# Latent attention in a two-layer decoder: rotation of all tokens of two heads on VectorE instead of GpSimd, rotary scores as stacked high and low parts, the causal mask by TensorE

## The chip, the core and the metric

One core of a Trainium2 chip runs the whole program in one launch. The metric is the device time of one execution in microseconds (us); the time before is the median of three runs. The core has TensorE (matrix products, `T` in the code, PE in the profile), VectorE (`V`, DVE), ScalarE (`A`, ACT), GpSimd (`G`, POOL) and SyncE (`Q`, SP), which issues most of the transfers. The engines run side by side, each working through its own queue in order.

## The reference

A sequence of 512 tokens of width 1024 goes through two layers, each of which is SwiGLU, a token mixer beside a memory cross-attention, and SwiGLU again. The mixer of the first layer is gated linear attention; that of the second is multi-head latent attention (MLA), and all of the change lies there:

```python
q = (rmsnorm(c_q, q_norm) @ w_uq).reshape(B, S, 8, 128 + 64)
kv = (rmsnorm(c_kv, kv_norm) @ w_ukv).reshape(B, S, 8, 128 + 128)
q_nope = rmsnorm(q[..., :128], qn_norm)
q_rope = apply_rope(rmsnorm(q[..., 128:], qr_norm), cos, sin)
k_nope = rmsnorm(kv[..., :128], kn_norm)
k_rope = apply_rope(rmsnorm(k_r, kr_norm)[:, :, None, :], cos, sin)   # one for all heads
# apply_rope: t1, t2 = halves of 32;  [t1*c - t2*s, t1*s + t2*c]
s = (q_nope k_nope + q_rope k_rope) * 192 ** -0.5;  causal mask;  softmax;  times v
```

All arithmetic is float32.

## The kernel before, in words

**Arithmetic.** Large products are made of float32r operands (a float32 rounded so that TensorE takes it in one pass): each operand is split into a high part and what is left (a low part), and `mm3` adds three products. Weights come by DMA as `raw`, ScalarE rounds them into `wh`, VectorE subtracts to make `wl`. Small products (attention scores, probabilities times values) use plain float32 operands; each such product stands in the trace as two matmul records.

**The MLA mixer** (`mla`, line 1387). The latents `cq`, `ck` and the raw rotary key `krn` come from token projections; `rope_tables` makes eight tables of cosines and sines times gains on GpSimd. `rope_key` (line 1437) rotates the key of all 512 tokens, copies it into both halves of 128 columns, and transposes it, so that `kr["t"]` holds it twice, on rows 0 to 63 and 64 to 127.

Then come four pairs of heads, pair 0 to pair 3. For each pair TensorE projects keys and values (four blocks of 128 tokens, 512 wide) and queries (four blocks, 384 wide: 256 without position, 128 rotary). `query` copies a block out of PSUM and sums its squares, `queries` (line 1477) waits for all four blocks, takes the inverse roots, and for each block j scales its two parts on VectorE and calls `rotate` (line 1373), six GpSimd instructions of 64 elements. Then each block takes three transposes, two for the heads and one for both rotary parts. `attend` (line 1540) makes the scores of one head and block j as a float32 product over 128 rows and a second one over the 64 rows of that head's rotary part, both `(j+1)*128` wide, and `attention` (line 1107) adds the mask to the diagonal block in PSUM on VectorE, takes the row maximum, the exponential on ScalarE, scales the rows, transposes, and multiplies by the values. When pair 2 is through its projections, `mem.attend`, the cross-attention into the memory tokens, is started too. After pair 3's projections the output projection `project_out` (line 873) begins with the first six heads: each of its eight outputs needs heads 0 to 5 in order, so it can't finish one before pair 2 is through its attention.

**What sets the order.** The kernel is written as generators ("flows"), and a planner (`Flows.run`, line 264) picks in each step the flow whose next instruction can start first by its own cost table (`Engine.price`, line 142). The order so found is fixed at build time: each engine's queue has it, and an instruction that waits holds up all behind it. The flows take temporary tiles from a pool of 33 tiles of 1024 columns, most of them as halves of 512 (`tt`), banks of PSUM from eight. All engine calls are made on line 138, so the profile's rows are told apart by tiles and shapes: `cs` with a PE row is the identity, so `ps<-cs,t` is a transpose; `t,wh` is the output projection or SwiGLU; `wh,t` with 384 or 512 columns is a pair's projection; `ps<-t` is attention; `cm` with a DVE row holds the mask, `s` are columns of sums.

Of the kernel before, what the change touches and what calls it, by code (L numbers as in the profile page):

```python
# [9 lines left out]
F32 = mybir.dt.float32  # L10
# [279 lines left out]
def _emit(tc, ctx, xT, memT, wflat, sizes, cst, out):  # L290
# [816 lines left out]
    def attention(scores, blocks, value, o, mask=None):  # L1107
# [265 lines left out]
    def rotate(dst, src, tabs, n):  # L1373

        tmp = yield tt()
        a, b, a2, b2 = (tmp[:, i * 128 : i * 128 + n].rearrange("p (x d) -> p x d", d=32) for i in range(4))
        c1, s1, c2, s2 = tabs
        t1, t2 = src[:, :, 0:32], src[:, :, 32:64]
        yield G.tensor_tensor(out=a, in0=t1, in1=c1, op=ALU.mult)
        yield G.tensor_tensor(out=b, in0=t2, in1=s2, op=ALU.mult)  # L1380
        yield G.tensor_tensor(out=dst[:, :, 0:32], in0=a, in1=b, op=ALU.subtract)
        yield G.tensor_tensor(out=a2, in0=t1, in1=s1, op=ALU.mult)
        yield G.tensor_tensor(out=b2, in0=t2, in1=c2, op=ALU.mult)
        yield G.tensor_tensor(out=dst[:, :, 32:64], in0=a2, in1=b2, op=ALU.add)
        done(tmp)

    def mla(l, nrm, nxt):
# [6 lines left out]
        yield from rope_tables(rt)  # L1394
        spawn(mem_prep(l, mem.mp))
# [41 lines left out]
        def rope_key():  # L1437
# [4 lines left out]
            yield from rotate(krd3[:, :, 0:ROPE], krn3, rt[4:8], 128)  # L1442
            yield G.tensor_copy(out=krd3[:, :, ROPE:], in_=krd3[:, :, :ROPE])
# [4 lines left out]
            kr["t"] = yield tt()  # L1448
            yield A.copy(out=kr["t"], in_=ps)
# [14 lines left out]
        def query(st, j, ps):  # L1464
            t = yield tt()
            yield A.copy(out=t[:, :384], in_=ps[:, :384])
# [7 lines left out]
            st["raw"][j] = t  # L1474
            st["f"][j].set = True

        def queries(st):
            for f in st["f"]:
                yield f
            ss, rc = st["ss"], small(16)  # L1480
            yield V.tensor_tensor(out=ss, in0=ss, in1=C("invq"), op=ALU.mult)
            yield from rsqrt(rc, ss, 1.0, 16)
            st["q"] = []
            for _ in range(3):
                st["q"].append((yield tt()))
            q0, q1, qr = st["q"]
            for j in range(NJ):
                qn = st["raw"][j]
                for c0, c1, dd, cc in ((0, 256, NOPE, 4 * j), (256, 384, ROPE, 4 * j + 2)):
                    q3 = heads(qn[:, c0:c1], 2)  # L1490
                    yield V.tensor_tensor(out=q3, in0=q3, in1=rc[:, cc : cc + 2].unsqueeze(2).to_broadcast([P, 2, dd]),
                                          op=ALU.mult)
                tabs = [rt[i][:, j, :].unsqueeze(1).to_broadcast([P, 2, 32]) for i in range(4)]
                yield from rotate(heads(qn[:, 384:512], 2), heads(qn[:, 256:384], 2), tabs, 64)
            for j in range(NJ):
                qn = st["raw"][j]
                pt = yield bank()
                for i, c0 in enumerate((0, 128, 384)):
                    yield T.transpose(out=pt[:, i * P : (i + 1) * P], in_=qn[:, c0 : c0 + P], identity=ident)
                done(qn)  # L1500
                sl = slice(j * P, (j + 1) * P)
                for i in range(2):
                    yield A.activation(out=st["q"][i][:, sl], in_=pt[:, i * P : (i + 1) * P], func=AF.Identity, scale=qns)
                yield V.tensor_copy(out=qr[:, sl], in_=pt[:, 2 * P : 3 * P])
                done(pt)
            st["qf"].set = True
# [11 lines left out]
        def keys(st):  # L1518
# [4 lines left out]
            st["k"] = []  # L1523
            for _ in range(2):
                st["k"].append((yield tt()))
            for j in range(NJ):
# [6 lines left out]
                for i in range(2):  # L1533
                    yield A.activation(out=st["k"][i][:, sl], in_=pt[:, i * P : (i + 1) * P], func=AF.Identity,
                                       scale=C("kn"))
# [4 lines left out]
        def attend(st, i, h):  # L1540
# [5 lines left out]
            rp = slice(i * ROPE, (i + 1) * ROPE)  # L1546

            def scores(ps, j):
                n = (j + 1) * P
                sl = slice(j * P, n)  # L1550
                yield T.matmul(ps[:, :n], lhsT=st["q"][i][:, sl], rhs=st["k"][i][:, :n], start=True, stop=False)
                yield T.matmul(ps[:, :n], lhsT=st["q"][2][rp, sl], rhs=kr["t"][rp, :n], start=False, stop=True)
# [253 lines left out]
```

## Time and profile before

| | us |
|---|---|
| median of three runs | 2018.53 (2016.92 to 2018.84) |
| profiled execution, its own time | 2016.53 |
| its span, first to last instruction | 2014.7 |
| PE busy in the span | 1999.7 |
| DVE busy | 1578.5 |
| ACT busy | 978.3 |
| POOL busy | 48.4 |

The span is one profiled execution. A row of instructions names line, engine, operation, out<-in tiles, shapes and count, then busy time and the mean duration of one in ns, then the idle time of the engine just before them with what ended it. Durations of matmuls overlap, so what one costs a full queue is read from start to start.

### The profile page before, as it was taken

The numbers are of one execution on the slowest core, as the hardware profiler recorded it, in microseconds if no ns is written. First come the engines' busy times: TensorE is split into PE (matmuls) and PEld (weight loads), VectorE is DVE, ScalarE is ACT, GpSimd is POOL, SyncE is SP. The second block draws the span as 40 slices with busy tenths as digits, with TensorE's granted clock in tenths as the row PEclk, the third lists the DMA queues.
The fourth block names the chain that finished last, engine by engine and source line by source line (L and its number), as shares of the span: only waits on it lengthen the run. The fifth ranks groups of instructions, "written<-read, shape, count | busy, mean of one in ns | idle before, by whom it ended". The sixth has DMA issues, their size and how long they took to land.

```text
span 2014.7 us, 32006 instructions
## 1 busy us (share of the span) xinstructions
PE 1999.7 (99%) x12862; PEld 1796.6 (89%) x12862; DVE 1578.5 (78%) x2573; ACT 978.3 (49%) x1574; POOL 48.4 (2%) x121
## 2 busy tenths in 40 slices
PE   9999999999999999999999999999999999999999
PEld 8999998878987899999899999989877779998997
DVE  8977786548776998678799777865887669987782
ACT  6543444444442664445565444444576456543451
POOL 0000000000000000000000000010031100000000
PEclk9999999999999999999999999999999999999999
DMA  5333333313212133323323333333210212332231
GB/s 180 108 108 102 105 105 112 108 63 105 74 57 79 64 97 114 115 86 104 126 96 105 105 105 100 101 115 111 87 45 32 84 43 84 105 128 92 95 126 63
DMA packets 55589, 193.22 MB, mean 96 GB/s; under 512 B 6160, under 2 KB 7824, under 8 KB 55440
## 3 DMA queue, kind: packets, MB, share of 16 engines
q1 hardware_dynamic: 55152, 189.92, 28.6%
q8 instruction: 101, 1.65, 0.3%
q10 hardware_dynamic: 288, 1.26, 0.2%
q14 instruction: 48, 0.39, 0.1%
HBM read 189.05 MB, written 2.10 MB: 95 GB/s over the span
## 4 chain that ended last, share of the span: by engine, by line
PE 87%; DVE 9%; ACT 2%; issue 1%; DMA 0%; POOL 0%; SPq 0%; ACTq 0%; DVEq 0%; POOLq 0%
PE ps L138 87%; DVE t L138 5%; DVE wl L138 2%; DVE s L138 2%; ACT t L138 1%; ACT wh L138 1%; DMA raw<-wflat 0%; DVE raw L138 0%; DVE x L138 0%; POOL t L138 0%; SPq L138 0%; DVE ps L138 0%; DVE rs L138 0%; ACTq L138 0%; DVEq L138 0%
## 5 line engine op out<-in xcount | busy, mean ns | idle before, releaser
L138 PE MATMUL ps<-t,wh 128*128 128x256 f32 (+1 forms) x6880 | 1528.0, 318 | 2.8 <-ACT wh L138 1.7
L138 PEld LDWEIGHTS ps<-t,wh 128*128 128x128 f32 x6880 | 1141.1, 191 | 96.0 <-issue 7.2
L138 PE MATMUL ps<-t,wl 128*128 128x256 f32 (+1 forms) x3440 | 1091.1, 317 | 0.1
L138 PEld LDWEIGHTS ps<-t,wl 128*128 128x128 f32 x3440 | 655.5, 191 | 45.6 <-issue 3.0
L138 ACT CAST wh<-raw 128x1024 fp32r<-128x1024 f32 (+2 forms) x358 | 368.6, 1031 | 483.8 <-PE ps L138 357.1
L138 DVE TENSOR_TENSOR wl<-raw,wh 128x1024 fp32r<-128x1024 f32 (+2 forms) x358 | 428.4, 1199 | 114.3 <-ACT wh L138 113.6
L138 DVE TENSOR_TENSOR t<-t 128x512 f32<-128x512 f32 (+3 forms) x514 | 306.5, 618 | 13.1 <-ACT t L138 8.4
L138 ACT CAST wh<-t 128x1024 fp32r<-128x1024 f32 x126 | 132.4, 1051 | 185.5 <-PE ps L138 98.9
L138 PE MATMUL ps<-wh,t 128*128 128x256 f32 (+3 forms) x928 | 214.9, 321 | 0.0
L138 DVE TENSOR_TENSOR wl<-t,wh 128x1024 fp32r<-128x1024 f32 x126 | 153.7, 1220 | 48.9 <-ACT wh L138 48.8
L138 DVE SCALAR_TENSOR_TENSOR x<-ps,x 128x512 f32<-128x512 f32 x160 | 109.8, 686 | 104.7 <-PE ps L138 104.6
L138 ACT COPY t<-ps 128x512 f32<-128x512 f32 (+3 forms) x262 | 138.8, 534 | 65.1 <-PE ps L138 58.5
L138 PEld LDWEIGHTS ps<-wh,t 128*128 128x128 f32 x928 | 155.1, 190 | 9.6 <-issue 2.2
L138 DVE TENSOR_TENSOR t<-ps,t 128x512 f32<-128x512 f32 (+2 forms) x191 | 122.6, 645 | 50.3 <-PE ps L138 36.0
L138 PE MATMUL ps<-wl,t 128*128 128x256 f32 (+3 forms) x464 | 148.2, 319 | 0.0
L138 PE MATMUL ps<-t 128*128 128x128 f32 (+6 forms) x760 | 139.7, 328 | 0.8 <-ACT t L138 0.4
L138 ACT CAST t<-t 128x256 fp32r<-128x256 f32 (+1 forms) x196 | 95.3, 509 | 78.8 <-DVE t L138 78.5
L138 PEld LDWEIGHTS ps<-t 128*128 128x128 f32 (+1 forms) x760 | 97.9, 190 | 30.4 <-issue 15.9
L138 DVE SCALAR_TENSOR_TENSOR t<-t 128x512 f32<-128x512 f32 (+1 forms) x168 | 106.0, 636 | 16.9 <-ACT t L138 16.2
L138 DVE TENSOR_TENSOR t<-t,raw 128x1024 f32<-128x1024 f32 x84 | 102.2, 1217 | 0.1
L138 ACT ACTIVATE t<-t 128x512 f32<-128x512 f32 x124 | 76.3, 629 | 48.1 <-DVE t L138 47.8
L138 PEld LDWEIGHTS ps<-wl,t 128*128 128x128 f32 x464 | 88.3, 190 | 4.9 <-issue 0.9
(76 smaller groups left out, 786.4 us busy)
## 6 DMA issues: line engine op xcount, KB each, us to landing
raw<-wflat SPq DMA_DIRECT2D x342, 512.0 KB, 3.3
raw<-wflat SPq DMA_DIRECT2D x12, 192.0 KB, 2.3
x<-xT SPq DMA_DIRECT2D x8, 256.0 KB, 5.6
t<-memT SPq DMA_DIRECT2D x8, 256.0 KB, 3.6
out<-x SPq DMA_DIRECT2D x8, 256.0 KB, 2.0
raw<-wflat SPq DMA_DIRECT2D x4, 448.0 KB, 3.3
cm<-cst ACTq DMA_DIRECT2D x1, 640.0 KB, 3.9
cm<-cst ACTq DMA_DIRECT2D x1, 585.5 KB, 4.2
```

The costliest lines, as they stand in the source:

```text
L138: return Op(self.name, lambda: real(*args, **kw), cost, _places(ins), _places(outs), lat)
```

## The change

- `rotate` runs on VectorE. It takes all four blocks of both heads of a pair in one call: four multiplications and two sums of 256 elements in place of 24 GpSimd instructions of 64. For the key it is six instructions of 128 elements, and the copy into the second half is VectorE's too.
- `query` puts the rotary parts of all blocks into one tile `st["rope"]`; one instruction reduces the six sums of a block, and the mean of a head's 128 columns is made from two sums of 64. The scaling of the rotary part is one instruction of 512 elements.
- The rotated queries are split into a rounded high part (ScalarE) and a low part (VectorE), which lie beside each other, 64 and 64 columns for each head, so that a transpose gives 128 rows: high above low. There are four transposes for a block in place of three.
- The rotated key is split into a pair of float32r tiles. The rotary score of a head is two float32r products over 128 rows, stacked query times high key and stacked query times low key, in place of one float32 product over 64 rows.
- The mask is added by a third product, identity times mask, 128 wide in float32r; the VectorE addition goes. Two casts at the start of `mla` make both operands.
- Both heads' queries and keys lie in whole tiles (`Take("d", ...)`), so that one ScalarE instruction of 256 elements scales both heads of a block; the VectorE copy of the rotary part is 256 wide instead of 128.

```diff
     def attention(scores, blocks, value, o):
         def rows(j, ps):
-            if mask is not None:
-                sl = slice(j * P, (j + 1) * P)
-                yield V.tensor_tensor(out=ps[:, sl], in0=ps[:, sl], in1=mask, op=ALU.add)
-    def rotate(dst, src, tabs, n):
-        yield G.tensor_tensor(out=a, in0=t1, in1=c1, op=ALU.mult)
...
-        yield G.tensor_tensor(out=dst[:, :, 32:64], in0=a2, in1=b2, op=ALU.add)
+    def rotate(dst, src, rt, n):
+        a, b = (t[:, : NJ * n * ROPE].rearrange("p (j h d) -> p j h d", j=NJ, h=n) for t in ab)
+        t1, t2 = src[:, :, :, 0:32], src[:, :, :, 32:64]
+        for out_, in_, i in ((a[:, :, :, 0:32], t1, 0), (b[:, :, :, 0:32], t2, 3), (a[:, :, :, 32:64], t2, 2),
+                             (b[:, :, :, 32:64], t1, 1)):
+            yield V.tensor_tensor(out=out_, in0=in_, in1=tab(i), op=ALU.mult)
+        yield V.tensor_tensor(out=dst[:, :, :, 0:32], in0=a[:, :, :, 0:32], in1=b[:, :, :, 0:32], op=ALU.subtract)
+        yield V.tensor_tensor(out=dst[:, :, :, 32:64], in0=a[:, :, :, 32:64], in1=b[:, :, :, 32:64], op=ALU.add)
     def mla(l, nrm, nxt):
+        yield V.tensor_copy(out=identr, in_=ident)
+        yield V.tensor_copy(out=maskr, in_=C("cmask"))
         def rope_key():
-            yield G.tensor_copy(out=krd3[:, :, ROPE:], in_=krd3[:, :, :ROPE])
+            yield V.tensor_copy(out=krd3[:, :, ROPE:], in_=krd3[:, :, :ROPE])
-            yield A.copy(out=kr["t"], in_=ps)
+            kr["t"] = yield from pair()
+            yield from split(ps, *kr["t"])
         def query(st, j, ps):
-            yield A.copy(out=t[:, :384], in_=ps[:, :384])
+            yield A.copy(out=t, in_=ps[:, :256])
+            yield A.copy(out=heads(st["rope"], NJ)[:, j, :], in_=ps[:, 256:384])
-            yield V.tensor_reduce(out=ss[:, 4 * j : 4 * j + 2], in_=heads(sq[:, :256], 2), op=ALU.add, axis=AX.X)
-            yield V.tensor_reduce(out=ss[:, 4 * j + 2 : 4 * j + 4], in_=heads(sq[:, 256:384], 2), op=ALU.add, axis=AX.X)
+            yield V.tensor_reduce(out=ss[:, 6 * j : 6 * j + 6], in_=heads(sq[:, :384], 6), op=ALU.add, axis=AX.X)
         def queries(st):
-                yield from rotate(heads(qn[:, 384:512], 2), heads(qn[:, 256:384], 2), tabs, 64)
+            yield V.tensor_tensor(out=q3, in0=q3, in1=rc6[:, :, 4:6].unsqueeze(3).to_broadcast([P, NJ, 2, ROPE]),
+                                  op=ALU.mult)
+            yield from rotate(ql, q3, rt, 2)
+            yield A.copy(out=qh.bitcast(F32R), in_=ql)
+            yield V.tensor_tensor(out=ql, in0=ql, in1=qh, op=ALU.subtract)
...
-                for i, c0 in enumerate((0, 128, 384)):
-                    yield T.transpose(out=pt[:, i * P : (i + 1) * P], in_=qn[:, c0 : c0 + P], identity=ident)
+                yield from transposes(pt, qn, 2)
+                for i in range(2):
+                    x = (2 * j + i) * P
+                    yield T.transpose(out=pt[:, (2 + i) * P : (3 + i) * P], in_=hl[:, x : x + P], identity=ident)
-                yield V.tensor_copy(out=qr[:, sl], in_=pt[:, 2 * P : 3 * P])
+                yield V.tensor_copy(out=heads(st["qr"], 2)[:, :, sl], in_=heads(pt[:, 2 * P :], 2))
             def scores(ps, j):
-                yield T.matmul(ps[:, :n], lhsT=st["q"][2][rp, sl], rhs=kr["t"][rp, :n], start=False, stop=True)
+                for part in range(2):
+                    yield T.matmul(ps[:, :n], lhsT=st["qr"][:, i * S + j * P : i * S + n], rhs=kr["t"][part][:, :n],
+                                   start=False, stop=False, skip_group_check=True)
+                yield T.matmul(ps[:, sl], lhsT=identr, rhs=maskr, start=False, stop=True, skip_group_check=True)
```

The planner's order moves with it. On TensorE, before, the transposes of pair 3's queries (`ps<-cs,t` in threes) and its first scores (`ps<-t`) stand inside the output projection (`t,wh` and `t,wl`, 512 wide):

```order
L138 MATMUL ps<-t,wh 128x512 x2
L138 MATMUL ps<-t,wl 128x512
L138 MATMUL ps<-cs,t 128x128 x3
L138 MATMUL ps<-t,wh 128x512 x2
L138 MATMUL ps<-cs,t 128x128 x3
L138 MATMUL ps<-t,wl 128x512
L138 MATMUL ps<-t,wh 128x512
L138 MATMUL ps<-t 128x128 x2
L138 MATMUL ps<-t 128x256 x2
```

By then heads 4 and 5 are done. On TensorE, now, it is pair 2's query transposes (in fours) that stand where pair 3's query projection (`wh,t`, 384 wide) ends and the output projection begins:

```order
L138 MATMUL ps<-cs,t 128x128 x4
L138 MATMUL ps<-wh,t 128x384 x2
L138 MATMUL ps<-wl,t 128x384
L138 MATMUL ps<-cs,t 128x128 x4
L138 MATMUL ps<-wh,t 128x384
L138 MATMUL ps<-t,wh 128x512 x2
L138 MATMUL ps<-cs,t 128x128 x4
L138 MATMUL ps<-t,wl 128x512
L138 MATMUL ps<-t,wh 128x512 x2
```

So pair 2's attention, pair 3's queries and attention and the cross-attention into the memory follow each other with 18 products of the output projection among them (its first output: 12 of heads 0 to 3, later 6 of heads 4 and 5), and the other outputs come after them.

On VectorE, before, pair 3's scores meet the mask (`ps<-ps,cm`) and the row maximum, one block after the other, late in the mixer:

```order
L138 SCALAR_TENSOR_TENSOR x_82<-ps,x_82 128x512
L138 COPY t<-ps 128x128
L138 TENSOR_TENSOR ps<-ps,cm 128x128
L138 TENSOR_REDUCE s<-ps 128x1
L138 TENSOR_TENSOR ps<-ps,cm 128x128 x2
L138 RECIPROCAL s<-s 128x1
L138 TENSOR_REDUCE s<-ps 128x1
L138 TENSOR_SCALAR t<-t,s 128x128
```

On VectorE, now, the rotation of pair 3 (`t<-t`, 8x32) and its scaling stand among the row maxima (`s<-ps`) and row scalings of pair 2's attention and of the memory's:

```order
L138 TENSOR_TENSOR t<-t,s_15421 128x512
L138 RECIPROCAL s<-s 128x2
L138 TENSOR_REDUCE s<-ps 128x2
L138 TENSOR_SCALAR t<-t,s 128x256 x2
L138 TENSOR_TENSOR t<-t 128x8x32 x4
L138 RECIPROCAL s<-s 128x2
L138 TENSOR_REDUCE s<-ps 128x1
L138 TENSOR_TENSOR t<-t 128x8x32
L138 TENSOR_TENSOR t<-ps,t 128x512
L138 TENSOR_TENSOR t<-t 128x8x32
```

The mask additions are gone from this queue, the rotation has come in, and what was GpSimd's lies behind VectorE's other work.

More of the change, by code (lines that the diff above doesn't have):

```diff
@@ L1104, in _emit, with attention @@
     xqs = const.tile([P, 2], F32, name="xqs")
-    def attention(scores, blocks, value, o, mask=None):
+    def attention(scores, blocks, value, o):
         po = yield bank(1)
@@ L1371, in rope_tables, with tab @@
         yield V.tensor_scalar_mul(out=qns, in0=C("qn"), scalar1=MSC)
-    def rotate(dst, src, tabs, n):
[L1375 to L1378, printed above, removed]
-        yield G.tensor_tensor(out=a, in0=t1, in1=c1, op=ALU.mult)
[L1380 to L1383, printed above, removed]
-        yield G.tensor_tensor(out=dst[:, :, 32:64], in0=a2, in1=b2, op=ALU.add)
-        done(tmp)
+    def rotate(dst, src, rt, n):
+        ab = []
+        for _ in range(2):
+            ab.append((yield tt()))
+        a, b = (t[:, : NJ * n * ROPE].rearrange("p (j h d) -> p j h d", j=NJ, h=n) for t in ab)
+        def tab(i):
+            return rt[i].unsqueeze(2).to_broadcast([P, NJ, n, ROPE // 2])
+        t1, t2 = src[:, :, :, 0:32], src[:, :, :, 32:64]
[4 more added lines that the diff above has]
+        yield V.tensor_tensor(out=dst[:, :, :, 32:64], in0=a[:, :, :, 32:64], in1=b[:, :, :, 32:64], op=ALU.add)
+        done(*ab)
     def mla(l, nrm, nxt):
@@ L1479, in queries @@
                 yield f
[L1480 to L1486, printed above, removed]
-            for j in range(NJ):
[L1488 to L1493, printed above, removed]
-                yield from rotate(heads(qn[:, 384:512], 2), heads(qn[:, 256:384], 2), tabs, 64)
+            ss, rc = st["ss"], sm.tile([P, 24], F32, tag="s6", name="s6", bufs=8)
@@ new lines, in queries @@
+            two = ss.rearrange("p (j b) -> p j b", j=NJ)[:, :, :4].rearrange("p j (h b) -> p j h b", h=2)
+            sums = small(8)
+            yield V.tensor_tensor(out=sums.rearrange("p (j h) -> p j h", j=NJ), in0=two[:, :, :, 0], in1=two[:, :, :, 1],
+                                  op=ALU.add)
+            for b in range(2):
+                yield V.tensor_scalar_mul(out=two[:, :, :, b], in0=sums.rearrange("p (j h) -> p j h", j=NJ), scalar1=0.5)
+            v, y, t = (sm.tile([P, 24], F32, tag="s6", name="s6", bufs=8) for _ in range(3))
@@ new lines, in queries @@
+            yield from newton_rsqrt(rc, ss, 1.0 / ROPE, v, y, t)
+            st["q"] = yield Take("d", F32, 0)
+            st["qr"] = yield Take("d", F32R, 0)
+            rc6 = rc.rearrange("p (j b) -> p j b", j=NJ)
+            q3 = heads(st["rope"], NJ).rearrange("p j (h d) -> p j h d", h=2)
+            yield V.tensor_tensor(out=q3, in0=q3, in1=rc6[:, :, 4:6].unsqueeze(3).to_broadcast([P, NJ, 2, ROPE]),
+                                  op=ALU.mult)
+            hl = yield Take("d", F32, 0)
@@ new lines, in queries @@
+            hl5 = hl.rearrange("p (j h c d) -> p j h c d", j=NJ, h=2, c=2)
+            qh, ql = hl5[:, :, :, 0, :], hl5[:, :, :, 1, :]
+            yield from rotate(ql, q3, rt, 2)
+            done(st["rope"])
+            qh, ql = (hl.rearrange("p (x c d) -> p x c d", c=2, d=ROPE)[:, :, c, :] for c in range(2))
+            yield A.copy(out=qh.bitcast(F32R), in_=ql)
+            yield V.tensor_tensor(out=ql, in0=ql, in1=qh, op=ALU.subtract)
+            for j in range(NJ):
+                q3 = heads(st["raw"][j], 4)
+                yield V.tensor_tensor(out=q3, in0=q3, in1=rc[:, 6 * j : 6 * j + 4].unsqueeze(2).to_broadcast([P, 4, ROPE]),
+                                      op=ALU.mult)
@@ L1522, in keys @@
             yield from rsqrt(rc, st["ks"], 1.0 / NOPE, 8)
-            st["k"] = []
-            for _ in range(2):
-                st["k"].append((yield tt()))
+            st["k"] = yield Take("d", F32, 0)
             for j in range(NJ):
@@ L1532, in keys @@
                 sl = slice(j * P, (j + 1) * P)
-                for i in range(2):
-                    yield A.activation(out=st["k"][i][:, sl], in_=pt[:, i * P : (i + 1) * P], func=AF.Identity,
-                                       scale=C("kn"))
+                yield A.activation(out=heads(st["k"], 2)[:, :, sl], in_=heads(pt[:, : 2 * P], 2), func=AF.Identity,
+                                   scale=C("kn"))
                 done(pt)
```

35 lines of the change are left out of this document (18 added, 17 removed).

## The prediction

> **What bounds the kernel now.** I read the page first: its busy times and its chain.
>
> ```profile
> span 2014.7 us, 32006 instructions
> PE 1999.7 (99%) x12862; PEld 1796.6 (89%) x12862; DVE 1578.5 (78%) x2573; ACT 978.3 (49%) x1574; POOL 48.4 (2%) x121
> PE 87%; DVE 9%; ACT 2%; issue 1%; DMA 0%; POOL 0%; SPq 0%; ACTq 0%; DVEq 0%; POOLq 0%
> ```
>
> TensorE is busy in all but 15 us of the span, and 87% of the chain that ended last is its own work. So a microsecond of TensorE work that goes is a microsecond gained unless a wait takes its place. GpSimd's 48.4 us are 2% and 0% of the chain: what they cost can only be seen where someone waits for them. Next comes the table of stretches, for the mixer that changes (columns: stretch, length, then busy time with count for PE, PEld, DVE, ACT, POOL).
>
> ```profile
> 1400.00:1460.00 60.00, 58.22 (x360) 51.90 (x359) 51.52 (x192) 33.77 (x76) 3.90 (x7) 1.00 0.30 91
> 1460.00:1500.00 40.00, 36.83 (x192) 29.43 (x191) 36.35 (x142) 30.93 (x96) 18.97 (x48) 1.00 0.18 57
> 1500.00:1560.00 60.00, 58.91 (x346) 42.65 (x346) 45.30 (x148) 38.66 (x121) 7.81 (x24) 1.00 0.08 28
> ```
>
> TensorE is idle for 1.78, 3.17 and 1.09 us here, 6.0 of the 15. The worst place is 1460 to 1500, where VectorE is busy for 36.35 of 40 us. The granted clock is 1.00 throughout. The list of waits of TensorE over the whole run says for whom:
>
> ```profile
> PE ps L138 <- ACT t L138: 3.4, 7, 0.8
> PE ps L138 <- POOL t L138: 1.2, 1, 1.2
> ```
>
> One wait of 1.2 us is for GpSimd (the key's rotation). The largest sum, 3.4 us over seven waits, is for ScalarE. So removing GpSimd's work is worth at most 1.2 us by itself; the rest has to come from TensorE's products, and VectorE, nearly full in 1460 to 1500, is what could give it back.
>
> **The change, part by part.**
>
> *The 64-row products go.* Groups by shape in 1280 to 1760 (two records for a product, 16 records for the eight heads), then TensorE's timeline:
>
> ```profile
> L138 PE MATMUL ps<-t 64*128 64x512 f32 x16 | 9.0, 641 | 0.0
> L138 PE MATMUL ps<-t 64*128 64x384 f32 x16 | 7.3, 535 | 0.0
> L138 PE MATMUL ps<-t 64*128 64x256 f32 x16 | 5.6, 428 | 0.0
> L138 PE MATMUL ps<-t 64*128 64x128 f32 x16 | 3.9, 322 | 0.0
> ```
>
> ```profile
> 1496.10 1.67 PE L138 MATMUL ps<-t 128*128 128x128 f32 x8
> 1496.86 0.91 PE L138 MATMUL ps<-t 64*128 64x384 f32 x2
> 1497.70 0.66 PE L138 MATMUL ps<-cs,t 128*128 128x128 f32 x4
> 1498.19 2.69 PE L138 MATMUL ps<-t 128*128 128x512 f32 x8
> 1499.76 1.12 PE L138 MATMUL ps<-t 64*128 64x512 f32 x2
> 1500.81 0.44 PE L138 MATMUL ps<-cs,t 128*128 128x128 f32 x2
> 1504.48 0.93 PE L138 MATMUL ps<-cs,t 128*128 128x128 f32 x7
> 1505.25 1.02 PE L138 MATMUL ps<-t 128*128 128x512 f32 x2
> ```
>
> From its start to the start of what follows, a 64x512 product takes 1.05 us (1499.76 to 1500.81) and a 64x384 one 0.84 (1496.86 to 1497.70). The means fall by 107 ns for each 128 columns and record, so two records fall by 0.21: 0.63 and 0.42 for the narrower two. A head has one of each, 2.94 us; eight heads, 23.5. The change of height costs more on both sides. Seven transposes take 0.77 us (1504.48 to 1505.25), 0.11 each. The six 128-row records of the group at 1496.10 take 0.76, 0.10 above that; the four transposes behind a 64-row product (1497.70 to 1498.19) take 0.49, 0.05 above it. That is 0.15 for each of 32 products, 4.8. Together 28.3 us of TensorE's queue go.
>
> [...]
>
> *What replaces them.* A table row and groups of two stretches full of float32r products, a piece of the timeline, and a group of products with one column:
>
> ```profile
> 1322.00:1342.00 20.00, 20.00 (x90) 16.57 (x89) 9.35 (x13) 6.98 (x10) 0.00 (x0) 1.00 0.29 95
> ```
>
> ```profile
> L138 PE MATMUL ps<-t,wh 128*128 128x256 f32 x90 | 16.4, 283 | 0.0
> L138 PE MATMUL ps<-t,wl 128*128 128x256 f32 x46 | 12.9, 283 | 0.0
> ```
>
> ```profile
> 1512.13 0.52 PE L138 MATMUL ps<-wh,t 128*128 128x384 f32 x2
> ...
> 1512.67 0.52 PE L138 MATMUL ps<-wh,t 128*128 128x384 f32 x2
> ```
>
> ```profile
> L138 PE MATMUL ps<-ones,t 128*128 128x1 f32 x8 | 0.9, 239 | 0.0
> ```
>
> At 512 columns 90 products take 20 us, 0.22 each; at 256, 136 take the 16 us of 1682 to 1698, 0.12; at 384, three take 0.54 (1512.13 to 1512.67, one of `wl` between), 0.18. Two per head and block: 8 x 2 x (0.22 + 0.18 + 0.12) = 8.3 us. At 128 columns no float32r product stands in the trace, and there will be 48: 16 of the first blocks and 32 masks. Records with a single column still take about 0.1 each (0.9 for eight), so lower than 0.10 is not to be had; the plain float32 product of that shape is two records of 0.11, 0.22, the upper bound. I take 0.11, from the transposes, which have the same 128x128 operands in one record: 5.3 us (4.8 to 10.6). Sixteen more transposes, 1.8. TensorE's queue: -28.3 + 8.3 + 5.3 + 1.8 = **-12.9** (-13.4 to -7.6). This lies on the path wherever TensorE isn't waiting.
>
> *VectorE's account.* Groups of 1465 to 1580; then the timeline, and the GpSimd rows of the rotation:
>
> ```profile
> L138 DVE TENSOR_TENSOR t<-ps,t 128x512 fp32r<-128x512 f32 x18 | 12.3, 687 | 6.8 <-ACT t L138 6.7
> L138 DVE TENSOR_TENSOR t<-t,s 128x256 f32<-128x256 f32 x23 | 10.0, 444 | 0.1
> L138 DVE TENSOR_REDUCE s<-t 128x2 f32<-128x256 f32 x22 | 9.0, 410 | 1.5 <-ACT t L138 1.5
> L138 DVE TENSOR_SCALAR t<-t,s 128x256 f32<-128x256 f32 x22 | 7.3, 354 | 0.3
> L138 DVE TENSOR_TENSOR ps<-ps,cm 128x128 f32<-128x128 f32 x24 | 7.1, 294 | 4.4 <-PE ps L138 4.2
> L138 DVE TENSOR_TENSOR t<-t,s 128x128 f32<-128x128 f32 x12 | 3.9, 327 | 0.0
> L138 DVE COPY t<-ps 128x128 f32<-128x128 f32 x12 | 3.4, 285 | 1.1 <-PE ps L138 0.9
> L138 DVE TENSOR_REDUCE s<-t 128x2 f32<-128x128 f32 x11 | 3.0, 274 | 0.0
> ```
>
> ```profile
> 1467.87 1.50 DVE L138 TENSOR_TENSOR t<-t,s 128x256 f32<-128x256 f32 x4
> 1469.29 1.34 DVE L138 TENSOR_TENSOR wl<-raw,wh 128x1024 fp32r<-128x1024 f32 x1
> ```
>
> ```profile
> L138 POOL TENSOR_TENSOR t<-t 128x64 f32<-128x64 f32 x96 | 35.3, 399 | 146.8 <-DVE t L138 107.2 <-PE ps L138 36.7 <-DVE s L138 2.1
> ```
>
> For a pair there go four reductions at 0.41 and four at 0.27, four scalings at 0.33, eight masks at 0.29, four copies at 0.29 and a small one at 0.17: 7.7 us. There come four reductions of 384 (0.55, between the rows of 256 and 512), three small ones, a scaling and a subtraction of 512 (0.69 each), six rotation steps of 256 and four copies of 256 (0.42 each): 8.3 us. So the rotation is nearly paid for by the masks: +0.6 a pair, 2.4 for four. The key adds seven of 128 columns (0.29), a split (0.69) and two casts: 3.3. VectorE gets some 6 us more of 270 in the mixer, and GpSimd's 35.3 and the key's share go. The key's part falls in 1400 to 1460, where VectorE has 8.5 us free; it removes the wait of **-1.2**. ScalarE's 64 scalings of 128 become 32 of 256, against four rounded copies and sixteen small ones; it has a fifth of its time free even in 1460 to 1500, so I cost it at nothing.
>
> *The order.* This costs more than the account. The order puts pair 2's attention, pair 3's queries and the memory's attention in one piece with only one output of the output projection in it. I counted VectorE's queue from the first reduction behind a score of the memory's attention to the last row scaling that a transpose of pair 2's last block waits for: 147 instructions, namely 4 of 1024 columns (1.3), 20 of 512 (0.69), 7 of 384 (0.55), 35 of 256 (0.42), 2 of 128 (0.29), 20 row scalings (0.35) and 59 small (0.17), 55.1 us of durations. They overlap: four of 256 start within 1.42 us (1467.87 to 1469.29), 0.355 each against 0.444, so 0.08 of each is shared; 55.1 - 11.8 = 43.3. TensorE has 251 products between the same two points: 72 transposes and 12 narrow products at 0.11, 70 of 256 at 0.12, 40 of 384 at 0.18, 40 of 512 at 0.22, and 17 plain ones at 0.21 for each 128 columns, 6.3: 40.0. TensorE must wait 3.3 there, and, by the same count, 1.0 in a shorter piece in pair 0's and pair 1's attention (61 instructions, 16.4 against 15.4): **+4.3**. That is with VectorE never idle. In 1460 to 1500, the one such piece now, TensorE lost 3.17 though VectorE's load was under its own, since the steps go to and fro through ScalarE; with one more such piece I add **+3.2**.
>
> *The port.* Of 1400 to 1465, when GpSimd mostly rests, the groups say:
>
> ```profile
> L138 DVE TENSOR_TENSOR t<-t,s 128x256 f32<-128x256 f32 x4 | 1.7, 418 | 0.0
> L138 DVE TENSOR_SCALAR s<-s 128x8 f32<-128x8 f32 x2 | 0.3, 172 | 0.1
> ```
>
> Beside the rotation the instruction of 256 takes 444, 0.026 more. If each of some 60 instructions of VectorE that now run beside the rotation grew by that, 1.5 us would come back; as one row of four instructions shows it, I leave that out of the sum. [...]
>
> Sum: -12.9 - 1.2 + 4.3 + 3.2 = **-6.6**. The profiled execution took 2016.53 us, 1.8 around its span, so 2009.9; it lies 2.0 below the median of 2018.53, so **2011.9**.
>
> **The rivals.** About 4 us, 0.2%, is what a measurement can tell from no change here.
>
> *Slower: VectorE's queue becomes the bound in the piece.* The 0.08 shared by neighbours holds where the next instruction waits for nothing. In the small chains of the inverse roots, and where each step waits for ScalarE, it doesn't. If all 208 counted instructions lose it, TensorE waits 16.6 more: -14.1 + 4.3 + 16.6 = +6.8, 2025.3. From 9.8 lost on it is no gain, from 13.8 on slower. For it: VectorE's 36.35 of 40 with 3.17 idle on TensorE. Against: chains of two pairs interleave, and the masks no longer stand between score and maximum. 0.12.
>
> *No change: the narrow float32r product costs 0.22.* TensorE then saves 7.6: -7.6 - 1.2 + 4.3 + 3.2 = -1.3, 2017.2. For it: no such row in the trace; the narrowest that it has is 256 wide. Against: records of one column cost 0.1, as if the weights set it. 0.25.
>
> *The whole gain.* The pieces hide behind TensorE, and the port is free: -12.9 - 1.2 - 1.5 = -15.6, 2002.9. For it: the softmax chain is a step shorter. Against: the count above. 0.20.
>
> **How the numbers follow.** The forecast has 0.43. It and the whole gain are faster: 0.63. The narrow product's case is the same: 0.25. VectorE's is slower: 0.12. The range reaches from the whole gain, 2003, past the case of no change to 2021, which leaves out most of the slower case.
>
> **What would show it.** The 64-row groups are gone, and 64 float32r products and 32 masks stand in their place; the narrow ones start 0.11 apart if I am right, 0.22 if the second rival is. TensorE's busy time falls by some 13 less what the waits are. In the piece before the output projection VectorE is full and TensorE idles for 5 to 8 us; over 14 us there, and the slower case is true. No wait for GpSimd is left. The forecast is wrong if SwiGLU's stretches change, or if the idle time of the mixer stays at 6 us.

## The result and the profile after

The changed kernel takes 2005.47 us (median of 4 runs, 2005.36 to 2005.65) against 2018.49: ratio 0.9939, 95% interval 0.9927 to 0.9952. A second set of runs beside the experiments gave 2005.48 against 2017.10, ratio 0.9941 (0.9928 to 0.9954). One run of that set (2411.61 us, mean granted clock 0.75) and one of mask_scale below (2136.24 us, 0.85) were slow and are left out of the medians. The other runs of the changed kernel lie between 2005.36 and 2006.06; those of the kernel before lie in two groups, near 2016.6 and near 2018.5; so the gain is 11 to 13 us by where the median of before falls. Between the two profiled executions, of 2016.53 and 2005.36 us, it is 11.2.

From the page of the changed kernel, its span, busy times and chain:

```profile
span 2003.6 us, 31893 instructions
PE 1987.7 (99%) x12910; PEld 1801.7 (90%) x12910; DVE 1575.5 (79%) x2559; ACT 975.6 (49%) x1562; POOL 9.2 (0%) x18
PE 88%; DVE 8%; ACT 2%; issue 1%; DMA 0%; SPq 0%; ACTq 0%; DVEq 0%
```

TensorE's busy time fell by 12.0 us (1999.7 to 1987.7), its idle time rose by 0.9 (15.0 to 15.9): together the 11.1 by which the span is shorter. So the gain is TensorE's queue, and hardly anything was given back in waits. Where the waits lie is in the table of stretches, first of the changed kernel, then the rows of before that the prediction did not show (columns as there: busy time and count of PE, PEld, DVE, ACT, POOL, then the granted clock):

```profile
1400.00:1460.00 60.00, 59.41 (x365) 52.79 (x364) 53.21 (x201) 34.35 (x82) 0.00 (x0) 1.00 0.29 91
1460.00:1500.00 40.00, 38.51 (x227) 32.80 (x226) 39.05 (x148) 31.80 (x93) 0.00 (x0) 1.00 0.19 57
1500.00:1560.00 60.00, 58.21 (x383) 50.49 (x382) 47.97 (x158) 42.53 (x125) 0.00 (x0) 1.00 0.20 63
1560.00:1600.00 40.00, 37.32 (x243) 31.17 (x242) 27.46 (x70) 22.21 (x57) 0.00 (x0) 1.00 0.04 14
1541.00:1568.00 27.00, 24.25 (x158) 19.99 (x157) 26.35 (x91) 18.94 (x57) 0.00 (x0) 1.00 0.18 59
1360.00:1660.00 300.00, 293.17 (x1746) 255.26 (x1745) 227.83 (x721) 175.09 (x444) 0.00 (x0) 1.00 0.22 69
```

```profile
1560.00:1600.00 40.00, 40.00 (x209) 32.85 (x208) 29.40 (x78) 20.52 (x43) 8.50 (x24) 1.00 0.25 80
1360.00:1660.00 300.00, 293.54 (x1630) 239.70 (x1629) 219.60 (x712) 168.80 (x440) 39.17 (x103) 1.00 0.21 67
```

The mixer's idle time on TensorE is 6.83 us after (300 less 293.17) and 6.46 before. But it has moved. From 1400 to 1500 it fell from 4.95 to 2.08 us. From 1500 to 1560 it rose from 1.09 to 1.79, and from 1560 to 1600, where before had none, it is now 2.68. The row 1541 to 1568 is the piece in which pair 2's attention, pair 3's queries and the memory's attention follow each other: VectorE is busy for 26.35 of 27 us there and TensorE idles for 2.75. The list of waits says the same:

```profile
PE ps L138 <- DVE t L138: 6.0, 11, 1.5
PE ps L138 <- ACT t L138: 2.1, 7, 0.4
```

No wait for GpSimd is left. Those for VectorE's tiles rose from 2.3 (the line of before below) to 6.0 us, those for ScalarE's fell from 3.4 to 2.1.

```profile
PE ps L138 <- DVE t L138: 2.3, 5, 1.3
```

### The profile page after: what moved, and what is told of

Its sections match the earlier page's. It is cut to its first block, busy times and chain, and to the rows that moved or that the text cites. A ratio compares the mean times of both kernels' runs of the same rounds, so it can differ in the third digit from the quotient of the medians.

```text
span 2003.6 us, 31893 instructions
## 1 busy us (share of the span) xinstructions
PE 1987.7 (99%) x12910; PEld 1801.7 (90%) x12910; DVE 1575.5 (79%) x2559; ACT 975.6 (49%) x1562; POOL 9.2 (0%) x18
## 4 chain that ended last, share of the span: by engine, by line
PE 88%; DVE 8%; ACT 2%; issue 1%; DMA 0%; SPq 0%; ACTq 0%; DVEq 0%
PE ps L138 88%; DVE t L138 4%; DVE s L138 2%; DVE wl L138 2%; ACT t L138 1%; ACT wh L138 0%; DMA x<-xT 0%; DVE x L138 0%; DVE raw L138 0%; SPq L138 0%; DVE rs L138 0%; ACTq L138 0%; DVEq L138 0%
## 5 line engine op out<-in xcount | busy, mean ns | idle before, releaser
L138 DVE TENSOR_TENSOR t<-t 128x512 f32<-128x512 f32 (+4 forms) x548 | 319.7, 605 | 13.9 <-ACT t L138 8.7
L138 PE MATMUL ps<-t 128*128 128x128 f32 (+5 forms) x792 | 129.8, 315 | 1.6 <-DVE t L138 0.8
L138 PEld LDWEIGHTS ps<-t 128*128 128x128 f32 (+1 forms) x792 | 103.3, 190 | 18.1 <-issue 5.3
```

The lines of the kernel that those rows point to most:

```text
L138: return Op(self.name, lambda: real(*args, **kw), cost, _places(ins), _places(outs), lat)
```

## The experiments

Theory 1: TensorE's queue carries the gain, above all through the 64-row products, and what is given back is given back where VectorE's queue is as long as TensorE's. The rivals: the gain needs float32r's single pass (one record a product in the trace, 0.22 us at 512 columns, where a plain float32 product is two records and takes 0.86 in pad128); or the waits come from how long the way to and fro through ScalarE or GpSimd is, not from VectorE's load. The runs stand on three chips, each with the kernel before beside it (its median 2016.78, 2017.10 and 2017.03 us). The order of each queue moves with every edit, so no run differs from another in the edited lines alone.

| run | us | less the kernel before | ratio (95%) | TensorE idle in the mixer |
|---|---|---|---|---|
| pad128 | 2006.22 | -10.6 | 0.9947 (0.9935 to 0.9960) | 6.45 |
| mask_on_v | 2003.17 | -13.6 | 0.9929 (0.9917 to 0.9942) | 5.60 |
| rot_on_pool | 2015.90 | -0.9 | 0.9993 (0.9984 to 1.0002) | 13.82 |
| mem_late | 2006.02 | -10.8 | 0.9945 (0.9932 to 0.9959) | 6.45 |
| changed_again | 2005.48 | -11.6 | 0.9941 (0.9928 to 0.9954) | 6.82 |
| scale_on_act | 2002.15 | -15.0 | 0.9924 (0.9912 to 0.9936) | 3.49 |
| rot_blocks_pool | 2022.75 | +5.7 | 1.0026 (1.0016 to 1.0037) | 17.82 |
| mask_scale | 2002.75 | -14.4 | 0.9926 (0.9913 to 0.9938) | 5.50 |
| extra_v | 2007.24 | -9.8 | 0.9950 (0.9938 to 0.9963) | 7.49 |
| before_scale_act | 2015.70 | -1.3 | 0.9992 (0.9984 to 1.0001) | 5.67 |
| before_rot_v | 2022.07 | +5.0 | 1.0022 (1.0013 to 1.0031) | 7.62 |
| pad_scale_act | 2008.76 | -8.3 | 0.9957 (0.9944 to 0.9969) | 6.76 |

### The 64-row products alone (pad128)

```diff
-            kr["t"] = yield tt()
-            yield A.copy(out=kr["t"], in_=ps)
+            for i in range(2):
+                t = yield tt()                      # rows lo: the key, rows hi: zeros
...
+                yield G.memset(t[hi], 0.0)
+                yield A.copy(out=t[lo], in_=ps[lo])
...
-                yield T.matmul(..., lhsT=st["q"][2][rp, sl], rhs=kr["t"][rp, :n], ...)
+                yield T.matmul(..., lhsT=st["q"][2][:, sl], rhs=kr["t"][i][:, :n], ...)
```

> The kernel before, with one edit: the rotary key is kept twice with the other half zeroed, so that each rotary score is a plain float32 product over 128 rows instead of 64; mask, rotation and stacking are as before. Theory 1 (what a 64-row product costs above a 128-row one, 0.21 us, and its two switches of height, 0.15, are TensorE time on the path): 32 x 0.36 = 11.5 us less, 2007, with the 16 wide records of a head now at 0.11 per 128 columns. Rival (the gain of the change needs float32r's single pass; the height of 64 costs nothing by itself): 2018.5, no change. Between the two, about 2013, if waits of TensorE for VectorE and ScalarE take back half.

Measured: 2006.22, 10.6 us less. Theory 1 holds, and the rival that single-pass float32r makes the gain falls. The mixer's row and a stretch of TensorE's timeline of this kernel:

```profile
1360.00:1660.00 300.00, 293.55 (x1694) 250.61 (x1694) 226.73 (x734) 176.77 (x456) 39.25 (x105) 1.00 0.22 69
```

```profile
1497.46 1.02 PE L138 MATMUL ps<-t 128*128 128x512 f32 x2
1498.32 0.38 PE L138 MATMUL ps<-cs,t 128*128 128x128 f32 x2
```

The idle time is that of before (6.45 against 6.46), so the whole gain is queue. Over 32 products 10.6 us are 0.33 each. A plain product over 128 rows and 512 columns takes 0.86 us from its start to that of the transposes behind it, where the one over 64 rows took 1.05: 0.19 of the 0.33; the rest fits the switches of height, which no run has by themselves. Zeros that double the arithmetic made the kernel faster.

### The mask back on VectorE (mask_on_v)

```diff
+            yield V.tensor_tensor(out=ps[:, sl], in0=ps[:, sl], in1=mask, op=ALU.add)
             yield V.tensor_reduce(out=nm, in_=ps[:, :n], op=ALU.max, axis=AX.X, negate=True)
...
-                yield T.matmul(ps[:, sl], lhsT=identr, rhs=maskr, start=False, stop=True, ...)
```

> The changed kernel, with the mask back on VectorE: 32 narrow products leave TensorE's queue, 32 additions of 128 columns (0.29 us each) come back on VectorE's, between score and row maximum. Theory 1 (VectorE's queue counted with its overlaps is the only thing that holds TensorE in the dense piece; counted on this kernel's order it gives the same stall, 4.9 against 4.8 us): 32 x 0.11 = 3.5 us less, 2002. Rival (the steps that go to and fro set the idle time, so a longer chain from score to maximum costs what the products saved): 2005 to 2009.

Measured: 2003.17, about 2.3 us below the changed kernel, and the longest of its five runs, 2003.70, is below the shortest of the changed kernel, 2005.36. So this part of the change is a loss. From its page and table of stretches:

```profile
span 2001.1 us, 31864 instructions
PE 1986.2 (99%) x12878; PEld 1799.5 (90%) x12878; DVE 1579.8 (79%) x2589; ACT 975.5 (49%) x1562; POOL 9.2 (0%) x18
```

```profile
1546.00:1548.00 2.00, 1.18 (x8) 1.09 (x8) 1.90 (x6) 2.00 (x7) 0.00 (x0) 0.86 0.00 0
1548.00:1550.00 2.00, 2.00 (x11) 2.00 (x11) 2.00 (x7) 0.44 (x2) 0.00 (x0) 0.50 0.43 133
1550.00:1552.00 2.00, 2.00 (x16) 1.87 (x14) 2.00 (x5) 1.35 (x5) 0.00 (x0) 0.79 0.33 129
```

There are 32 records fewer on TensorE and its busy time is 1.5 us lower, although it ran at half its clock for 3.4 us, which lost (0.14 + 0.50 + 0.21) x 2 = 1.7: 3.2 us of work went, 0.10 for each narrow product, as forecast. VectorE took the additions with less idle time on TensorE, not more.

### The queries' rotation back on GpSimd (rot_on_pool, rot_blocks_pool)

```diff
-            yield from rotate(ql, q3, rt, 2)              # VectorE
+            yield from rotate(ql, q3, rt, 2, G)           # rot_on_pool: six steps of 256 elements a pair
+            for j in range(NJ):                           # rot_blocks_pool: 24 of 64, then rounding and
+                yield from rotate(..., 2, G, 1)           # subtraction by blocks
+                yield A.copy(out=h5[:, j].bitcast(F32R), in_=l5[:, j])
+                yield V.tensor_tensor(out=l5[:, j], in0=l5[:, j], in1=h5[:, j], op=ALU.subtract)
```

> The changed kernel, with the six rotation steps of a pair's queries on GpSimd in the new form (256 elements each); the key's rotation stays on VectorE. 24 steps of 0.42 us leave VectorE's queue, ten us in all. Theory 1 (VectorE's queue is the bound in the dense piece): the counted stall falls from 4.8 to 1.8 us, 2002.5. Rival 1 (the way through GpSimd is longer and the first transposes of a pair wait for it, at 0.4 us and more a step than now): 2006 to 2010. Rival 2 (GpSimd's work slows VectorE's neighbours, 0.03 us each): 2005 to 2007, with longer VectorE means beside the rotation.

Measured: 2015.90, 10 us above the changed kernel; rival 1, and more than it said. GpSimd's, ScalarE's and TensorE's timelines at pair 0:

```profile
1468.12 5.60 POOL L138 TENSOR_TENSOR t<-t 128x256 f32<-128x256 f32 x6 [147.39 <-DVE t L138]
```

```profile
1473.75 0.62 ACT L138 CAST t<-t 128x512 fp32r<-128x512 f32 x1 [4.32 <-POOL t L138]
```

```profile
1475.67 0.48 PE L138 MATMUL ps<-wh,t 128*128 128x512 f32 x1
1480.47 0.66 PE L138 MATMUL ps<-cs,t 128*128 128x128 f32 x2 [4.32 <-DVE t L138]
```

The rotation takes 5.6 us, and ScalarE's rounding waits for it for 4.32 us with all that is queued behind it: copies and squares that VectorE and then TensorE need. Some microseconds on, TensorE waits 4.32 us, and the list of waits puts it down to VectorE. The rival had the way right; that it passes through ScalarE's queue was not in it. Rival 2 has a part too: VectorE's scalings of 256 elements in 1460 to 1500 took 530 ns here against 417 in the changed kernel. How much of the 10 us that is, no run separates.

> The changed kernel, with the queries' rotation on GpSimd by blocks, 24 instructions of 64 elements for a pair as in the kernel before, and rounding and subtraction by blocks behind it. All rotation of a pair on GpSimd at once cost 10 us more. If that was because no block could go on before six steps of 0.93 us were done, the first block now waits for six of 0.4 us, as before the change, and the time comes back to 2005 to 2007. If any way over GpSimd is what costs, through its longer steps and VectorE's slower ones beside it, 2010 or more.

Measured: 2022.75; the thought that the batch was to blame falls. From the table of stretches of this kernel:

```profile
1360.00:1660.00 300.00, 282.18 (x1648) 243.25 (x1648) 209.38 (x675) 164.54 (x432) 32.36 (x96) 0.98 0.21 67
```

TensorE idles for 17.82 us, 11 more than in the changed kernel, and a clock of 0.98 over 300 us is some 6 us more: these two make the 17 by which it is slower. By blocks there are also four roundings on ScalarE that wait for GpSimd instead of one.

### The memory's attention one step later (mem_late)

```diff
-            if p == 2:
+            if p == 3:
                 spawn(mem.attend())
```

> The changed kernel, with the memory's attention started after the last pair's projections instead of after the third pair's; no instruction is added or removed. Theory 1 (the idle time of the dense piece comes from VectorE's queue there): the counted stall falls from 4.8 to 3.5 us, so 2004; VectorE's share in the tightest 10 us falls with it. Rival (the idle time comes from steps that go to and fro, however they are spread): within 1 us of 2005.5, or slower as the work before the last outputs thickens.

Measured: 2006.02, the same as the changed kernel. Theory 1's 1.3 us did not come. In 1541 to 1568 VectorE was relieved but TensorE idled no less, 3.06 us; yet that is no longer the whole dense piece, which has moved forward. From 1530 to 1555 VectorE is full:

```profile
1541.00:1568.00 27.00, 23.94 (x167) 19.94 (x165) 24.18 (x87) 17.62 (x54) 0.00 (x0) 1.00 0.13 40
1530.00:1555.00 25.00, 22.51 (x142) 19.29 (x140) 25.00 (x91) 18.45 (x53) 0.00 (x0) 1.00 0.20 64
```

So TensorE's idle time still stands where VectorE is full, or just behind; a reordering of the same work moved it and did not remove it, and the count of the stall was wrong for this order.

### The changed kernel again (changed_again)

> The changed kernel itself, so that it, the kernel before and the other three kernels of this call stand on one chip. The medians so far differ by 13.0 us (2018.5 to 2005.5), the profiled executions by 11.2 (2016.53 to 2005.36). If the kernel before has two levels, 2016.5 and 2018.5, as its 15 runs beside the first four experiments look, and the changed one has not, the difference here is 11 to 13 by which of them the median falls on. If the chips differ instead, both medians shift alike.

Measured: 2005.48 against 2017.10, 11.6 us. The kernel before has the two groups on every chip, the changed one has one. No profile of the upper group was taken; what the listed clocks say of it stands in the last section.

### The row scaling on ScalarE (scale_on_act, mask_scale, before_scale_act, pad_scale_act)

```diff
-            yield V.tensor_scalar_mul(out=pr[:, :n], in0=pr[:, :n], scalar1=rc)
+            yield A.activation(out=pr[:, :n], in_=pr[:, :n], func=AF.Identity, scale=rc)
```

> The changed kernel, with the scaling of the probabilities' rows by the inverse sums (32 instructions of 128 to 512 columns, 0.28 to 0.49 us on VectorE, some 12 us in all) on ScalarE in the same place. Theory 1 (VectorE's queue length is what TensorE waits for in the dense piece): the counted stall falls from 4.8 to 2.3 us: 2.5 us less. Rival (what TensorE waits for is the length of the way from score to transpose, and ScalarE's step is no shorter, about 0.6 us for 512 columns and with another queue to wait in): the same time within 1 us, or up to 3 us longer.

Measured: 2002.15 (2001.91 to 2002.40), 3.3 us below the changed kernel on the same chip, the fastest of all kernels here. Its rows:

```profile
1541.00:1568.00 27.00, 26.21 (x169) 21.20 (x168) 24.34 (x83) 22.12 (x61) 0.00 (x0) 1.00 0.19 59
1360.00:1660.00 300.00, 296.51 (x1771) 258.22 (x1769) 222.07 (x696) 192.59 (x483) 0.00 (x0) 1.00 0.22 70
```

In the dense piece VectorE's load fell from 26.35 to 24.34 us and TensorE's idle time from 2.75 to 0.79; over the mixer 3.3 us of idle time went, the whole gain. The step that was moved got longer, as the rows of 1540 to 1570 show, first of the changed kernel, then of this one:

```profile
L138 DVE TENSOR_SCALAR t<-t,s 128x512 f32<-128x512 f32 x2 | 1.0, 482 | 0.0
```

```profile
L138 ACT ACTIVATE t<-t,s 128x512 f32<-128x512 f32 x2 | 1.5, 738 | 0.0
```

So the gain can't come from a shorter step: theory 1 holds here and its rival doesn't.

> The changed kernel with the mask on VectorE and the row scaling on ScalarE, together. The mask on VectorE alone gave 2003.2. Theory 1 (VectorE's queue): the counted stall is 5.3 against 4.9 us, so 2003.5. Rival (the way from score to transpose): longer than with the mask alone, 2004 to 2006. If the two add as separate gains, 2000.5.

Measured: 2002.75, with the mask on VectorE as well. The two gains don't add: 3.2 us of narrow products go, but the mask is again in VectorE's queue, and the profiled execution lost 1.7 us to a half clock as above.

> The kernel before, with the row scaling on ScalarE, the same edit that gave 3.5 us in the changed kernel. Theory 1 (VectorE's queue is a bound only in the dense piece that the changed order makes): the counted stall here is 1.3 us and falls to 0, so at most 1.3 us less, 2016 to 2017. Rival (ScalarE is the better place for it anywhere): 3 us less or more, 2014.

Measured: 2015.70, 1.3 less, with an interval that reaches to no change (1.0001); idle time in the mixer fell by 0.8 us. That is theory 1's side: without a dense piece there is little to relieve.

> The kernel before with 128-row rotary products (zeros in the other half of the key) and the row scaling on ScalarE; rotation and mask stay on GpSimd and VectorE. TensorE's queue by theory 1 is 2.0 us longer than the changed kernel's, and VectorE's counted stall is gone: the 128-row products alone gave 2006.2, so 2005 to 2006. If the scaling on ScalarE brings its 3.5 us here too: 2002.7.

Measured: 2008.76, 2.5 us above pad128, a miss for both. Its table of stretches:

```profile
1492.00:1494.00 2.00, 0.74 (x3) 0.34 (x3) 2.00 (x7) 1.72 (x8) 1.98 (x5) 1.00 0.00 0
1494.00:1496.00 2.00, 1.69 (x5) 0.98 (x6) 1.10 (x6) 2.00 (x9) 0.32 (x1) 0.66 0.00 0
1496.00:1498.00 2.00, 2.00 (x7) 1.29 (x6) 0.29 (x2) 1.29 (x5) 0.00 (x0) 0.50 0.00 0
1498.00:1500.00 2.00, 2.00 (x17) 1.99 (x16) 0.77 (x3) 1.69 (x6) 0.00 (x0) 0.99 0.00 0
```

Idle time is up by 0.3 us only. But the clock fell to half behind a stretch in which TensorE was busy for 0.74 of 2 us: 1.7 of the 2.5 us. The rest is open.

### More work in VectorE's queue (extra_v)

```diff
             yield V.tensor_scalar_mul(out=pr[:, :n], in0=pr[:, :n], scalar1=rc)
+            yield V.tensor_scalar_mul(out=spare[0][:, :n], in0=spare[1][:, :n], scalar1=0.5)
```

> The changed kernel, with one more VectorE scaling behind each row scaling, of the same width, from a table into a tile that nobody reads: 32 instructions, some 12 us more in VectorE's queue, no step longer in any chain by itself. Theory 1 (VectorE's queue is what TensorE waits for in the dense piece): the mirror of the row scaling on ScalarE, which gave 3.5 us; the counted stall rises from 4.8 to 7.5 us, so 2 to 4 us more than the changed kernel's 2005.6. Rival (the row scaling on ScalarE gained through its place there and not through VectorE's queue): within 1 us of 2005.6.

Measured: 2007.24, 1.8 us more than the changed kernel's 2005.48. But this isn't the mirror of scale_on_act. In the trace all 32 extra scalings stand between 1365 and 1383, a hundred us ahead of the attention. VectorE's groups of 1360 to 1400, where the changed kernel has none of these:

```profile
L138 DVE TENSOR_SCALAR t<-t 128x512 f32<-128x512 f32 x8 | 3.4, 424 | 0.1
L138 DVE TENSOR_SCALAR t<-t 128x384 f32<-128x384 f32 x8 | 2.9, 359 | 0.1
L138 DVE TENSOR_SCALAR t<-t 128x256 f32<-128x256 f32 x8 | 2.4, 295 | 0.2
L138 DVE TENSOR_SCALAR t<-t 128x128 f32<-128x128 f32 x8 | 1.8, 223 | 0.1
```

An instruction that reads nothing the attention makes did not stay behind the row scaling where the code has it; what put it forward isn't on record, so a queue needn't have the order in which the planner made its calls. In 1541 to 1568 VectorE is busy for 25.69 us, no more than in the changed kernel. The run tests neither theory 1 nor its rival, and what its 1.8 us are is open: idle time in the mixer rose by 0.7 of them.

### Rotation on VectorE in the kernel before (before_rot_v)

```diff
-    def rotate(dst, src, tabs, n):
+    def rotate(dst, src, tabs, n, G=G):
...
-                yield from rotate(heads(qn[:, 384:512], 2), heads(qn[:, 256:384], 2), tabs, 64)
+                yield from rotate(heads(qn[:, 384:512], 2), heads(qn[:, 256:384], 2), tabs, 64, V)
```

> The kernel before, with the queries' rotation on VectorE in its old form, 24 instructions of 64 elements for a pair. Theory 1 (the way from the inverse roots to the rotated queries over GpSimd, 0.4 us a step, is part of what TensorE waits for in pair 0 and pair 1): about half as long a way, 1 to 3 us less, 2014 to 2016. Rival (VectorE's queue is the bound there): 24 instructions of 0.2 us a pair come into it, the counted stall rises from 1.3 to 3.5 us: 2 us more, 2019.

Measured: 2022.07, 5.0 more; the rival's side. The table of stretches and TensorE's timeline of this kernel:

```profile
1475.00:1480.00 5.00, 5.00 (x25) 4.16 (x24) 5.00 (x26) 3.87 (x13) 0.00 (x0) 1.00 0.28 82
1495.00:1500.00 5.00, 2.35 (x8) 1.68 (x9) 4.85 (x30) 3.64 (x14) 0.00 (x0) 0.70 0.00 0
1500.00:1505.00 5.00, 5.00 (x21) 4.02 (x20) 2.26 (x10) 1.85 (x6) 0.00 (x0) 0.50 0.01 2
1505.00:1510.00 5.00, 4.38 (x25) 3.41 (x23) 3.85 (x19) 4.36 (x18) 0.00 (x0) 0.78 0.00 0
```

```profile
1496.97 1.09 PE L138 MATMUL ps<-cs,t 128*128 128x128 f32 x4 [3.19 <-DVE t L138]
```

VectorE gets behind in pair 0's attention (busy for 4.85 of 5 us from 1495 on) and TensorE waits 3.19 us for it. Idle time rises by only 1.2 us over the mixer (7.62 against 6.46); the clock loses (0.30 + 0.50 + 0.22) x 5 = 5.1. Together 6.3, the difference of the spans. The old form puts 24 steps of 0.22 us for a pair into VectorE's queue, the new one six of 0.42. Yet one thing improved: in 1475 to 1480 TensorE is never idle.

## Why the prediction was right or wrong

**The direction and the range** were right: 2011.9 forecast, 2003 to 2021 given, 2005.5 measured. The forecast's change of -6.6 us is half of the 13.0 between the medians and three fifths of the 11.2 between the profiled executions. About 2 us of the miss are the profiled execution of before, which lay in the lower of its two groups; the changed kernel has only one, so that the step from a span to the median carried 2.0 us over that weren't there.

**TensorE's queue, -12.9:** measured -12.0 as busy time. Of the 28.3 us of the 64-row products, pad128 tests the part by which such a product costs more than one over 128 rows: 10.6 less where 11.5 were counted. The narrow float32r product took 0.10 where 0.11 was taken, so the second rival (0.22) is out.

**The key's wait for GpSimd, -1.2:** gone, as forecast.

**VectorE's queue in the dense piece, +3.3:** 2.75 us of idle time at a VectorE busy for 26.35 of 27 us, 3.01 from 1530 to 1570. scale_on_act shows that VectorE's queue is its cause; mem_late shows that counting the queue doesn't give its size in another order.

**The steps that failed** are two waits: "a shorter piece in pair 0's and pair 1's attention", +1.0, and "with one more such piece I add +3.2". With +3.3 and the key's -1.2, TensorE's idle time was to rise by 6.3 us; it rose by 0.9 over the span and by 0.4 in the mixer (6.46 to 6.83). From 1460 to 1540 it fell, from 3.83 to 2.42, and the 3.01 of the dense piece are no more than VectorE's count alone had given. By the prediction's own test, "if the idle time of the mixer stays at 6 us", this part of it was wrong.

The +3.2 had copied the 3.17 us that TensorE lost in 1460 to 1500 before, which the prediction explained with "the steps go to and fro through ScalarE". By the single waits that holds for half. One wait of 1.33 us is for VectorE's scaling of the keys. The others (0.27 for VectorE, 0.64 and 0.77 for ScalarE) stand at the first softmax of pair 0, where ScalarE loads a table for 1.28 us ahead of its first exponential; the changed kernel has one wait of 1.48 us at the same place. So of the 3.17 us this second half stayed and the first went. Here is the first, with VectorE's scaling, in before; the same two in before_rot_v; and the second half, with the table load, in the changed kernel:

```profile
1476.65 0.41 DVE L138 TENSOR_TENSOR t<-t,s 128x256 f32<-128x256 f32 x1
1477.20 0.41 PE L138 MATMUL ps<-cs,t 128*128 128x128 f32 x2 [1.33 <-DVE t L138]
```

```profile
1477.16 0.42 DVE L138 TENSOR_TENSOR t<-t,s 128x256 f32<-128x256 f32 x1
1478.12 0.38 PE L138 MATMUL ps<-cs,t 128*128 128x128 f32 x2
```

```profile
1480.65 1.28 ACT L138 ACT_TABLE_LOAD   x1 [1.13 <-DVE s L138]
1483.50 0.30 PE L138 MATMUL ps<-cs,t 128*128 128x128 f32 x1 [1.48 <-DVE t L138]
```

The first wait didn't go because VectorE was done sooner: in before_rot_v the keys are scaled 0.5 us later than in before. TensorE's order there has eight more products of 512 columns ahead of the keys' transposes, and it is still busy with them. In the changed kernel the small steps that lead to the keys' scaling take 11.9 us from first to last, against 5.0 in before and 5.8 in before_rot_v, and TensorE has pair 0's transposes and scores to do meanwhile.

What GpSimd had to do with it is less clear. VectorE's groups in 1460 to 1500, before, then changed, then before_rot_v:

```profile
L138 DVE SCALAR_TENSOR_TENSOR s<-s 128x8 f32<-128x8 f32 x13 | 3.0, 232 | 0.2
```

```profile
L138 DVE SCALAR_TENSOR_TENSOR s<-s 128x8 f32<-128x8 f32 x12 | 1.9, 159 | 0.0
```

```profile
L138 DVE SCALAR_TENSOR_TENSOR s<-s 128x8 f32<-128x8 f32 x15 | 2.4, 163 | 0.1
```

Beside GpSimd's rotation the small steps of the keys' inverse roots took 232 ns (198 in pad128), without it 159 to 163: 13 of them at 0.07 more are 0.9 us of VectorE's queue. Whether TensorE's 1.33 us would have been shorter without that, in the order of before, no run shows, since none changes GpSimd's work and keeps the order. The mask had no part in it: in mask_on_v 1460 to 1500 is as good as in the changed kernel (38.65 us busy against 38.51).

**The port, left out of the sum,** stays open. It is the author's estimate of 1.5 us, from 444 ns for an instruction of 256 beside the rotation against 418 while GpSimd mostly rests; the whole gain's sum has it too. No run shows a port, or the 1.5 us by itself. Idle time in 1460 to 1500 fell by 1.7 (3.17 to 1.49); but 1.33 of that is the wait above, which the order took away, so the agreement is no evidence. What the runs show are durations: those of the small steps above, and in 1460 to 1500 the scalings of 256 took 440 ns in before against 417 in the changed kernel, while VectorE's reductions of 256 took 408 against 413. What that cost TensorE no run shows.

**The rivals.** The slower one fell: VectorE kept its overlap well enough (three rotation steps of 256 from 1469.21 on start 0.33 us apart in the changed kernel, at 417 ns each), and no run had 16.6 us more of waits; the most, 11.0 more than the changed kernel, has rot_blocks_pool. The whole gain, 2002.9, came nearer to the 2005.5 than the forecast did: of its queue's 12.9 us 12.0 came, and in place of 2.7 us of waits gone there are 0.9 more. It is also about what scale_on_act reaches with one more edit (-15.0 where it said -15.6). The range held because it reached down to this rival.

## What to carry to other kernels

Look for products over 64 rows among products over 128: here each cost 0.33 us more than one padded with zeros, and the padding alone gave 10.6 of the 11.6 us, without any of the rewriting. Before idle time of one stretch is carried over to another, take it apart wait by wait, and ask of each whether the new order still has it: 1.33 of the 3.17 us here went with the order. Where VectorE is full while ScalarE isn't, move a whole step of the chain (3.3 us here), but test parts of a change apart: the mask on TensorE cost 2.3 us that the others hid. And after an experiment that adds work to a queue, look in the trace for where the work went: in extra_v it went where nobody waited.

## What the runs showed of the hardware that was not expected

Behind stretches in which TensorE waited for much of the time, its granted clock fell to 0.50. TensorE had been busy for 0.15 of 4 us in rot_on_pool (1476 to 1480), 1.62 of 4 in pad_scale_act (1490 to 1494) and 0.93 of 2 in mask_scale (1482 to 1484), and 1.7 us were lost in each of these and in mask_on_v, which is 3.4 us at 0.50. In before_rot_v it was three times that length in a row (5.1 us lost), in rot_blocks_pool 6.8 us in three places. A plain product of 384 columns took 1.28 us from its start to what follows in pad_scale_act's slow stretch (1496.35 to 1497.63), 0.65 in pad128 at a clock of 1.00. So a wait can cost more in slow products than by itself: in before_rot_v 1.2 us of idle time went with 5.1 us of clock. In mask_on_v no single long wait stood ahead: the waits were of under 1 us each, in a stretch in which TensorE was busy for 2.23 of 4 us (1543 to 1547); its timeline there:

```profile
1545.79 0.30 PE L138 MATMUL ps<-cs,t 128*128 128x128 f32 x1 [0.95 <-DVE s L138]
1546.91 0.49 PE L138 MATMUL ps<-t 128*128 128x128 f32 x2 [0.82 <-ACT t L138]
```

The kernel before idled for 1.73 of 5 us in 1490 to 1495 (3.27 busy) and kept its clock at 1.00 in the profiled execution. Its upper group of runs is probably this drop: 3.4 us at half the clock would lower the mean over 2015 us by 0.0008 (an estimate from the 1.7 us above), and of its 49 runs beside the experiments all of the upper group, longer by about 1.8 us, list 0.999, all of the lower one 1.000. In mask_on_v and mask_scale too the single run that lists 1.000 is the shortest, by 1.2 and 1.3 us. In which stretch the upper group loses it isn't shown, as none of its runs was profiled.
